# First attention by halves of its heads, block-diagonal keys in every score product, early weight rounding on ScalarE

## Chip, cores and metric

One core of a Trainium2 chip runs the kernel in one launch. The metric is the device time of an execution in microseconds (us).

## What is computed

A row of 256 positions and 1,024 features goes through two layers of a first block and two layers of a second, all in float32. The first block's layer 0 is an attention of 16 heads of 64 with a relative bias, its layer 1 a gated spatial mixing (gMLP); each is followed by a squared-ReLU feed-forward of 4,096. Shift, scale and gate of each come from a conditioning vector `c` through `ada_w` (6 × 1,024 columns per layer). The second block's layers hold, side by side, a differential attention (4 heads, two score maps of 64 each) and a grouped one (8 query heads, 2 key heads of 64).

```python
def first_block(...):
    for i in range(DEPTH):
        sh1, sc1, g1, sh2, sc2, g2 = split(silu(c) @ ada_w[i] + ada_b[i], 6)
        h = rms_norm(x, norm_mix[i]) * (1 + sc1) + sh1
        y = chunked_relpos_attention(h, ...) if i == 0 else chunked_spatial_gating(h, ...)
        x = x + g1 * y
        h = rms_norm(x, norm_ffn[i]) * (1 + sc2) + sh2
        x = x + g2 * (square(relu(h @ w1[i])) @ w2[i])

# attention: q, k, v = split(h @ w_in, 3); q, k normed per head of 64
#   s = q @ k.T + bias (chunks of 64, no later chunk); o = softmax(s) @ v; o @ w_out
# second block, per layer: proj = h @ w_in_2[l]
#   differential: a = softmax(q0 k0.T + bias) - lam * softmax(q1 k1.T + bias); a @ v
#   grouped: softmax(q k.T) @ v with 4 query heads to a key head; then @ w_out_2, norm, x + ...
```

## The kernel before, in words

**Products.** A float32 product is taken as three matmuls of rounded parts (`mm3`, L771 to L773): high by high, high by low, low by high. `mm` (L759) is a plain float32 matmul, which the chip runs as two records. `tr` (L799) is a transpose.

**Weights.** All weights lie in one stream, cut into items of 128 × 1,024 (0.5 MB), two items to a group; `stream_items` sets their order. `load_group` (L831) loads groups on the SP queue into four raw buffers. `item` then takes an item up: a weight for products is rounded to its high part (`hi`, L870 on ScalarE or L871 on VectorE) and VectorE subtracts for the low part (L873); the pair takes 2,048 columns of the rounded arena `R` (25,856 columns). `place` gives a pair out only while fewer than `NHL` = 9 live and `R` has 2,048 + `SPARE` columns free. Items `adc` and `adg` of `ada_w` go through VectorE alone (L737, L729).

**Order.** Each phase records operations with their dependencies; `Sched` then plays them on a model of the engines and writes one fixed order per engine, so a changed program moves instructions everywhere. An operation with two choices (`hi`, copies out of PSUM, scaled copies) goes to the engine that the planner picks. Four rounds are played and the best one is built.

**First stage** (`attention`). For each of eight k: two `adc` items give the scale and shift of 128 features, ScalarE forms h, `split` makes its high and low parts, and eight `mm3` of 512 columns add to eight PSUM banks (queries and keys of all 16 heads, two row tiles). Then v in two halves, the norms of all heads, and 16 heads one by one: a transposed query and key block per two heads, scores, softmax, transpose, times v. A head is 64 rows of a 128-row block, so its two score products (L759) use 64 rows. Last the output projection with the residual, then the transposes for the feed-forward layer (`norm_T`).

**Last two layers** (`block2`). Queries and keys of the differential heads come transposed out of `ws_block`; a head's two maps sit in rows 0 to 63 and 64 to 127 of one block, and each score product is an `mm3` over 64 rows and 256 columns. The grouped heads do the same with one key block for the two key heads. Projections of v and of the gates are meant to fill TensorE between the heads.

Of the kernel before, what the change touches and what calls it, by code (L numbers as in the profile page):

```python
# [13 lines left out]
ALU = mybir.AluOpType  # L14
# [44 lines left out]
def stream_items():  # L59
    s = []  # L60
    for k in range(KT):
        s += [("adc", 0, 1, k), ("adc", 0, 0, k), ("aqk", k, 0), ("aqk", k, 1)]
    s += [("av", h, q) for h in range(2) for q in range(4)]
    for x, y in ((ada_items(0, (2,)), ada_items(0, (4,))), (ada_items(0, (3,)), [("ao", k) for k in range(KT)])):
        for p in zip(x, y):
            s += p
# [28 lines left out]
def item_array(it, a):  # L95
# [7 lines left out]
    if n == "aqk":  # L103
        return a["a_w_in"][0][it[1] * P:(it[1] + 1) * P, it[2] * D:(it[2] + 1) * D]
    if n == "av":
        _, h, q = it
        w = a["a_w_in"][0][q * 256:(q + 1) * 256, 2 * D + h * 512:2 * D + (h + 1) * 512]
        return w.reshape(2, P, 512).transpose(1, 0, 2).reshape(P, D)
# [216 lines left out]
class Sched:  # L325
    AHEAD = 300
    NHL = 9
    SPARE = 2048
# [65 lines left out]
    def schedule(self, spaces, slots, rounds=4):  # L394
# [4 lines left out]
        for i in range(rounds):  # L399
            out = self.round(spaces, slots)  # L400
# [244 lines left out]
class Prog:  # L645
# [188 lines left out]
    def item(self):  # L834
# [30 lines left out]
        else:  # L865
# [4 lines left out]
            self.prev_split = S.op([("ACT", 0.093 + D / 1200.0, lambda: nc.scalar.copy(out=res(hi), in_=res(src))),  # L870
                                    ("DVE", 0.068 + D / 1920.0, lambda: nc.vector.tensor_copy(out=res(hi), in_=res(src)))],  # L871
                                   [src], [hi], after=after, pri=pri, kind=("hi", it))
# [100 lines left out]
    def split(self, hi, lo, src, n, psum=False, scale=1.0):  # L973
# [6 lines left out]
            [src, hi], [lo], kind="split_lo")  # L980

# [135 lines left out]
    def attention(self):  # L1117
# [3 lines left out]
        def load_bias(pri):  # L1121
            last = self.prev_dma
            for i in range(4):
# [5 lines left out]
        self.hooks[POS["adg", 0, 2, 0] // GRP] = [load_bias]  # L1129
# [21 lines left out]
        qk = [[self.F(D) for _ in range(2)] for _ in range(2)]  # L1151
        acc = {(t, n): self.bank((4 * t + n,)) for t in range(2) for n in range(4)}
        for k in range(KT):
            self.w("aqk", k, 0)
# [5 lines left out]
            for n, j in ([(n, j) for j in range(2) for n in range(2)] if k < KT - 1 else [(0, 0), (0, 1), (1, 0), (1, 1)]):  # L1160
                w = self.w("aqk", k, j)
                for t in range(2):
                    sl = slice(n * 512, (n + 1) * 512)
                    self.mm3(acc[t, 2 * j + n].v(), h0(k, t), (w[0][:, sl], w[1][:, sl]), 512, k == 0, k == KT - 1)
        for c in range(2):
            for t in range(2):
                for j in range(2):
                    self.copy(qk[t][j].v(c)[:, c * 512:(c + 1) * 512], acc[t, 2 * j + c].v(), 512, psum=True)
        v = [self.F(D) for _ in range(2)]

        def v_half(h):
            names = [("av", h, q) for q in range(4)]
            ps = [self.bank((0, 1, 2, 3)) for _ in range(2)]
            for k in range(KT):
                q, r = divmod(k, 2)
                w = self.w(*names[q])
                sl = slice(r * 512, (r + 1) * 512)
                for t in range(2):
                    self.mm3(ps[t].v(), h0(k, t), (w[0][:, sl], w[1][:, sl]), 512, k == 0, k == KT - 1)
            for t in range(2):  # L1180
                self.copy(v[t].v(h)[:, h * 512:(h + 1) * 512], ps[t].v(), 512, psum=True)

        v_half(0)
        S.bias += 400
        v_half(1)
        S.bias -= 400

        for n in range(2):
            hs = slice(n * 512, (n + 1) * 512)
            for t in range(2):  # L1190
                sq, ssq = self.F(D), self.F(16)
                for w in range(2):
                    self.act(sq.v(w)[:, w * 512:(w + 1) * 512], qk[t][w].v(n)[:, hs], 512, AF.Square)
                self.red(ssq.v(), sq.v().r("p (h d) -> p h d", h=16), D, ALU.add)
                r = self.rsqrt(ssq.v(), 16, 1.0 / 64, newton=True)
                for w in range(2):
                    v3 = qk[t][w].v(n)[:, hs].r("p (h d) -> p h d", h=8)
                    self.tt(v3, v3, r.v()[:, w * 8:(w + 1) * 8].u(2).bc(P, 8, 64), 512, ALU.mult)
        gqk = self.F(1)
        self.stt(gqk.v(), self.col("gq"), -0.125, self.col("gk"), 1, ALU.mult, ALU.mult)  # L1200
        self.load_group(POS["adg", 0, 2, 0] // GRP)
# [6 lines left out]
        qT, kT = {}, {}  # L1208
        osb = {}
        for h in range(16):  # L1210
            blk = h // 2
            if h % 2 == 0:
                ps = self.bank(TB)
                self.tr([ps.v()[:, (2 * w + t) * P:(2 * w + t + 1) * P] for w in range(2) for t in range(2)],
                        [qk[t][w].v(blk // 4)[:, blk * P:(blk + 1) * P] for w in range(2) for t in range(2)])
                qT[blk], kT[blk] = self.F(256), self.F(256)
                self.act(qT[blk].v(), ps.v()[:, 0:256], 256, scale=gqk.v(), psum=True, dve=True)
                self.copy(kT[blk].v(), ps.v()[:, 256:512], 256, psum=True)
            rr = slice((h % 2) * 64, (h % 2) * 64 + 64)
# [5 lines left out]
            for t, c, bc in ((1, slice(0, 256), slice(0, 256)), (0, slice(256, 384), slice(128, 256))):  # L1225
                n = c.stop - c.start
                self.ttr(p.v(t)[:, c], ps.v()[:, c], bias[:, bc], n, 3e38, ALU.add, ALU.min, m.v(t)[:, t:t + 1])
# [10 lines left out]
            vh = slice(h * 64, h * 64 + 64)  # L1238
            o = (h % 4) * 64
            key = h // 8  # L1240
            self.mm(ob.v()[:, 256 + o:320 + o], pT.v()[:, 0:P], v[0].v(key)[:, vh], 64, True, False)
            self.mm(ob.v()[:, 256 + o:320 + o], pT.v()[:, P:256], v[1].v(key)[:, vh], 64, False, True)
            self.mm(ob.v()[:, o:o + 64], pT.v()[:, 256:384], v[0].v(key)[:, vh], 64, True, True)
# [116 lines left out]
    def block2(self, l):  # L1360
# [3 lines left out]
        if l == 0:  # L1364
            self.nd = [self.F(2 * 384) for _ in range(2)]
# [72 lines left out]
        for c, sc in ((AQ, -0.125), (AK, 1.0)):  # L1438
            for i in range(4):
                ps = self.ws_block(hT, ("ws", l, c + 128 * i), (0, 1, 2, 3))  # L1440
                aT[c, i] = self.R(256), self.R(256)
# [10 lines left out]
        bkT = self.R(256), self.R(256)  # L1452
        self.split(bkT[0].v(), bkT[1].v(), ps.v()[:, 0:256], 256, psum=True)
# [22 lines left out]
        for t in range(2):  # L1476
            ob = self.bank(OB)
            for h in range(4):
                p, m, w = self.F(512), self.F(2), self.F(1)
                for c in range(2):  # L1480
                    ps = self.bank(SB)
# [5 lines left out]
                    self.ttr(pc, ps.v()[:, 0:256], self.nd[h // 2].v()[:, o:o + 256], 256, 3e38, ALU.add, ALU.min,  # L1487
# [27 lines left out]
        for t in range(2):  # L1515
            ob = self.bank(OB)
            for i in range(4):
                p, m = self.F(512), self.F(2)
                for g in range(2):
                    ps = self.bank(SB)  # L1520
                    rr = slice(g * 64, g * 64 + 64)
# [112 lines left out]
```

## Time and profile before

| what | value |
|---|---|
| median of 3 runs | 1012.61 us (1011.96 to 1013.88) |
| profiled execution, its own time | 1012.26 us |
| its span, first to last instruction | 1009.8 us |
| HBM read | 214.48 MB |
| DMA engines, mean busy share of q1 | 56.0% |
| chain that ended last | PE 82%, DVE 11%, ACT 3%, DMA 2% |

PE is TensorE's matmul, PEld its weight load, DVE VectorE, ACT ScalarE, POOL GpSimd, SP the queue that loads weights. Busy time is the time covered by instructions; a matmul's end is modelled and reaches beyond the start of the next, so the pace of TensorE is read from the starts. The profiled execution's own time is 2.5 us longer than its span, by what lies around it.

### The profile page before, as it was taken

What the parts mean: (1) busy time and instruction counts of PE and PEld (TensorE: products, weight loads), DVE (VectorE), ACT (ScalarE), POOL (GpSimd) and SP (SyncE); (2) the same over time, 40 slices, a digit from 0 to 9 for tenths busy, and PEclk for the clock granted to TensorE, in tenths of its full rate; (3) what the DMA queues carried; (4) which work ended last, traced back from release to release, by engine and by line L of the source; (5) the groups of instructions that cost most, each with busy time, mean ns of one, the idle gap of its engine ahead of it and who ended that gap; (6) DMA issues with size and microseconds to landing.
All of it is one profiled execution on the core that took longest, in us unless ns stands there. A gap on an engine that the chain in (4) does not pass through costs nothing.

```text
span 1009.8 us, 15115 instructions
## 1 busy us (share of the span) xinstructions
PE 984.2 (97%) x5844; PEld 856.1 (85%) x5844; DVE 767.9 (76%) x1319; ACT 576.7 (57%) x1045; POOL 18.5 (2%) x36
## 2 busy tenths in 40 slices
PE   6999988999999999999999999999999999999997
PEld 5887777899999888999998899999889788897786
DVE  6999999999778976876667855565696666985753
ACT  6376846545455656744445744455474576854873
POOL 0001000000000000000000000010000000000000
PEclk9999998999999999999999999999999999999999
DMA  9994595999776495776543545575455242453101
GB/s 351 368 369 168 209 374 191 359 377 342 276 289 222 159 370 202 299 253 247 195 181 134 200 167 188 187 271 176 164 188 187 87 154 84 167 208 126 43 1 42
DMA packets 32119, 216.50 MB, mean 214 GB/s; under 512 B 3824, under 2 KB 4080, under 8 KB 7216
## 3 DMA queue, kind: packets, MB, share of 16 engines
q1 hardware_dynamic: 30816, 211.98, 56.0%
q0 software_dynamic: 1232, 3.56, 1.4%
q8 instruction: 46, 0.75, 0.3%
q14 instruction: 25, 0.20, 0.1%
HBM read 214.48 MB, written 1.05 MB: 213 GB/s over the span
## 4 chain that ended last, share of the span: by engine, by line
PE 82%; DVE 11%; ACT 3%; DMA 2%; issue 2%; SPq 0%; DVEq 0%; ACTq 0%
PE banks L771 25%; PE banks L773 24%; PE banks L772 24%; PE banks L759 5%; DVE arena_r L873 4%; PE banks L799 3%; DVE arena L729 2%; DVE arena L737 2%; DMA raw<-in_wall 1%; ACT arena L684 1%; DVE arena L710 1%; DVE arena_r L978 1%; ACT arena_r L870 1%; DVE arena_r L871 1%; ACT arena L699 0%
## 5 line engine op out<-in xcount | busy, mean ns | idle before, releaser
L771 PE MATMUL banks<-arena_r 128*128 128x512 f32 (+2 forms) x1664 | 569.0, 345 | 3.3 <-ACT arena_r L976 3.0
L772 PE MATMUL banks<-arena_r 128*128 128x512 f32 (+2 forms) x1664 | 554.3, 336 | 0.0
L773 PE MATMUL banks<-arena_r 128*128 128x512 f32 (+2 forms) x1664 | 553.9, 335 | 0.4 <-DVE arena_r L978 0.4
L873 DVE TENSOR_TENSOR arena_r<-raw,arena_r 128x1024 fp32r<-128x1024 f32 x300 | 362.8, 1222 | 91.5 <-ACT arena_r L870 88.4
L870 ACT CAST arena_r<-raw 128x1024 fp32r<-128x1024 f32 x270 | 281.2, 1047 | 182.7 <-PE banks L773 77.8
L771 PEld LDWEIGHTS banks<-arena_r 128*128 128x128 f32 (+1 forms) x1664 | 313.8, 190 | 47.8 <-issue 7.9
L773 PEld LDWEIGHTS banks<-arena_r 128*128 128x128 f32 (+1 forms) x1664 | 313.6, 190 | 34.3 <-DVE arena_r L978 1.8
L772 PEld LDWEIGHTS banks<-arena_r 128*128 128x128 f32 (+1 forms) x1664 | 314.3, 190 | 28.8
L684 ACT ACTIVATE arena<-arena 128x256 f32<-128x256 f32 (+8 forms) x160 | 66.4, 422 | 47.5 <-DVE arena L737 17.4
L976 ACT ACTIVATE arena_r<-arena 128x256 fp32r<-128x256 f32 (+1 forms) x120 | 55.9, 475 | 51.6 <-DVE arena L729 35.2
L759 PE MATMUL banks<-arena 128*128 128x64 f32 (+4 forms) x480 | 72.3, 292 | 5.0 <-DMA arena<-in_ident 3.8
L737 DVE CUSTOM_DVE_ANT_0 arena<-raw,arena 128x1024 f32<-128x1024 f32 x56 | 71.8, 1281 | 6.6 <-DMA raw<-in_wall 3.8
L759 PEld LDWEIGHTS banks<-arena 128*128 128x128 f32 (+1 forms) x480 | 62.8, 195 | 14.7 <-ACT arena L699 4.2
L684 ACT ACTIVATE arena<-banks 128x256 f32<-128x256 f32 (+1 forms) x104 | 44.7, 431 | 51.7 <-PE banks L773 49.9
L799 PE MATMUL banks<-arena 128*128 128x128 f32 x356 | 57.0, 285 | 11.1 <-ACT arena L958 4.9
L978 DVE SCALAR_TENSOR_TENSOR arena_r<-arena,arena_r 128x256 fp32r<-128x256 f32 (+1 forms) x120 | 58.1, 492 | 9.7 <-ACT arena_r L976 9.1
L699 ACT COPY arena<-banks 128x512 f32<-128x512 f32 (+2 forms) x93 | 46.0, 502 | 32.4 <-PE banks L799 16.7
L799 PEld LDWEIGHTS banks<-arena 128*128 128x128 f32 x356 | 43.5, 148 | 21.3 <-ACT arena L958 6.3
L710 DVE TENSOR_TENSOR arena<-arena 128x512 f32<-128x512 f32 (+6 forms) x128 | 51.4, 434 | 7.2 <-ACT arena L684 5.8
L729 DVE SCALAR_TENSOR_TENSOR arena<-raw,arena 128x1024 f32<-128x1024 f32 x40 | 51.3, 1282 | 6.6 <-DMA raw<-in_wall 6.2
L729 DVE SCALAR_TENSOR_TENSOR arena<-banks,arena 128x256 f32<-128x256 f32 (+1 forms) x84 | 37.9, 451 | 21.9 <-PE banks L759 13.1
L710 DVE TENSOR_TENSOR arena<-banks,arena 128x512 f32<-128x512 f32 (+1 forms) x48 | 29.8, 642 | 16.4 <-PE banks L773 7.5
(44 smaller groups left out, 315.7 us busy)
## 6 DMA issues: line engine op xcount, KB each, us to landing
raw<-in_wall SPq DMA_DIRECT2D x194, 1024.0 KB, 4.9
raw<-in_wall SPq DMA_DIRECT2D x8, 512.0 KB, 9.1
arena<-in_nbias SPq DMA_DIRECT2D x4, 512.0 KB, 8.3
arena<-in_rows POOLq DMA_DIRECT2D x3, 512.0 KB, 6.8
arena<-in_xin SPq DMA_DIRECT2D x2, 512.0 KB, 5.7
out_dram<-arena SPq DMA_DIRECT2D x4, 256.0 KB, 2.5
arena<-in_dbias POOLq DMA_DIRECT2D x2, 384.0 KB, 6.4
arena<-in_wsT POOLq DMA_DIRECT2D x1, 512.0 KB, 3.8
```

Source lines behind the costliest of these rows:

```text
L684: nc.scalar.activation(out=res(out), in_=res(in_), func=func, scale=res(scale), **kw, **({"accum_out": res(accum)} if accum is not None el ...
L710: alt = ("DVE", 0.068 + n / 960.0, lambda: nc.vector.tensor_tensor(out=res(out), in0=res(a), in1=res(b), op=op))
L729: return self.S.op(("DVE", dur, lambda: nc.vector.scalar_tensor_tensor(out=res(out), in0=res(a), scalar=res(s), in1=res(b), op0=op0, op1=o ...
L737: return self.S.op(("DVE", dur, lambda: nc.vector.tensor_tensor_reduce(out=res(junk if out is None else out), in0=res(a), in1=res(b), scal ...
L759: o = self.S.op(("PE", max(n, 96) * 0.00167, lambda: nc.tensor.matmul(res(out), lhsT=res(l), rhs=res(r), start=start, stop=stop)), rd, [ou ...
L771: nc.tensor.matmul(o, lhsT=lh, rhs=rh, start=start, stop=False)
L772: nc.tensor.matmul(o, lhsT=lh, rhs=rl, start=False, stop=False)
L773: nc.tensor.matmul(o, lhsT=ll, rhs=rh, start=False, stop=stop)
L799: nc.tensor.transpose(res(o), res(i), res(ident))
L870: self.prev_split = S.op([("ACT", 0.093 + D / 1200.0, lambda: nc.scalar.copy(out=res(hi), in_=res(src))), ("DVE", 0.068 + D / 1920.0, lamb ...
L873: dve = ("DVE", 0.068 + D / 960.0, lambda: nc.vector.tensor_tensor(out=res(lo), in0=res(src), in1=res(hi.f32()), op=ALU.subtract))
L978: self.S.op(("DVE", 0.068 + n / 960.0, lambda: nc.vector.scalar_tensor_tensor(out=res(lo), in0=res(src), scalar=scale, in1=res(hi.f32()), ...
```

## The change

1. *First attention by halves of heads.* In the k loop only the first eight heads' queries, keys and values are projected (six `mm3` per k and three banks per row tile). Items `aqk` hold both halves' 512 columns, `a2` the values and the second half. The second half's three projections are recorded between the first half's norms and its heads, with a priority that lets them fill in (`S.bias`). The bias tables load two and two.
2. *Block-diagonal keys.* Two 64-row key blocks are written into the two diagonal blocks of a 128 × 512 buffer whose other blocks are zeroed once. One product over 128 rows gives the scores of two heads (or of two maps). In `block2` the ten buffers of 512 columns are fixed in `R`; maxima of the grouped heads are taken for two heads at once.
3. *Early roundings.* Items ahead of the first feed-forward weight are rounded on ScalarE alone.
4. *Planner.* `SPARE` 2,048 to 5,120; a round that finds no operation to start ends the search.

```diff
-        s += [("adc", 0, 1, k), ("adc", 0, 0, k), ("aqk", k, 0), ("aqk", k, 1)]
-    s += [("av", h, q) for h in range(2) for q in range(4)]
+        s += [("adc", 0, 1, k), ("adc", 0, 0, k), ("aqk", k)]
+        if k % 2 == 0:
+            s.append(("a2", 2, 0, k // 2))
+    for x, y in ((ada_items(0, (2, 4)), [("a2", j, 1, q) for j in range(3) for q in range(4)]),
+                 (ada_items(0, (3,)), [("ao", k) for k in range(KT)])):
...
-    SPARE = 2048
+    SPARE = 5120
...
+            self.prev_split = S.op(alts[:1] if i < POS["w1", 0, 0] else alts, [src], [hi], after=after, pri=pri,
+                                   kind=("hi", it))
...
+    def split_diag(self, kd, ps):
+        for c in range(2):
+            rr, cc = slice(c * 64, c * 64 + 64), slice(c * 256, (c + 1) * 256)
+            self.split(kd[0].v(c)[rr, cc], kd[1].v(c)[rr, cc], ps.v()[rr, 0:256], 256, psum=True)
...
+        norms(0)
+        S.bias += 300
+        for j in range(3):
+            second(j)
+        S.bias -= 300
...
-            self.mm(ps.v()[:, 0:256], qT[blk].v()[rr, P:256], kT[blk].v()[rr, :], 256, True, True, 0.5)
-            self.mm(ps.v()[:, 256:384], qT[blk].v()[rr, 0:P], kT[blk].v()[rr, 0:P], P, True, True, 0.5)
+                self.mm(s1.v(), qT.v()[:, P:256], kk.v(), 512, True, True)
+                self.mm(s0.v()[:, 0:256], qT.v()[:, 0:P], kk.v().r("p (g k) -> p g k", g=2)[:, :, 0:P], 256, True, True)
...
+            self.kd = [(self.R(512), self.R(512)) for _ in range(5)]
...
-                    ps = self.bank(SB)
-                    rr = slice(c * 64, c * 64 + 64)
-                    self.mm3(ps.v()[:, 0:256], tuple(b.v()[rr, t * P:(t + 1) * P] for b in aT[AQ, h]),
-                             tuple(b.v()[rr, :] for b in aT[AK, h]), 256, True, True, 0.5)
+                ps = self.bank(SB)
+                self.mm3(ps.v(), tuple(b.v()[:, t * P:(t + 1) * P] for b in aT[AQ, h]), tuple(b.v() for b in self.kd[h]),
+                         512, True, True)
...
+                self.red(m.v(), ps.v().r("p (g k) -> p g k", g=2), 512, ALU.max)
```

What the planner makes of it, engine by engine. Lines of the changed kernel stand 10 or 11 lower: L739 is the old L729, L747 the old L737, L769 the old L759, L781 to L783 the old L771 to L773, L809 the old L799, L884 the old L873, L989 the old L978.

VectorE in the middle of the k loop, before (L737 takes an `adc` item, L729 of one column its gain, L871 rounds, L873 subtracts, L978 is the low part of h):

```order
L729 SCALAR_TENSOR_TENSOR arena<-arena 128x1
L871 CAST arena_r<-raw 128x1024
L873 TENSOR_TENSOR arena_r<-raw,arena_r 128x1024 x2
L978 SCALAR_TENSOR_TENSOR arena_r<-arena,arena_r 128x256
L737 ISA arena<-raw,arena 128x1024
L737 ISA arena 128x1
L737 ISA arena<-raw,arena 128x1024
```

The same place in the changed kernel:

```order
L739 SCALAR_TENSOR_TENSOR arena<-arena 128x1
L884 TENSOR_TENSOR arena_r<-raw,arena_r 128x1024
L989 SCALAR_TENSOR_TENSOR arena_r<-arena,arena_r 128x256
L747 ISA arena<-raw,arena 128x1024
L747 ISA arena 128x1
L747 ISA arena<-raw,arena 128x1024
L747 ISA arena 128x1
L884 TENSOR_TENSOR arena_r<-raw,arena_r 128x1024
```

The rounding is gone from VectorE, and a step holds one or two subtractions in place of two.

TensorE where the scores of the first `block2` layer begin, before (the products of 256 columns are scores over 64 rows, those of 512 columns projections):

```order
L799 MATMUL banks<-arena 128x128 x2
L771 MATMUL banks<-arena_r 128x256
L772 MATMUL banks<-arena_r 128x256
L773 MATMUL banks<-arena_r 128x256
L771 MATMUL banks<-arena_r 128x512
L772 MATMUL banks<-arena_r 128x512
L773 MATMUL banks<-arena_r 128x512
```

The same place in the changed kernel:

```order
L809 MATMUL banks<-arena 128x128 x2
L781 MATMUL banks<-arena_r 128x512
L782 MATMUL banks<-arena_r 128x512
L783 MATMUL banks<-arena_r 128x512
L781 MATMUL banks<-arena_r 128x512
L782 MATMUL banks<-arena_r 128x512
L783 MATMUL banks<-arena_r 128x512
```

No product of 256 columns is left among the heads: scores are as wide as the projections between them.

TensorE at the end of the first stage, before (L759 of one column sums the shift of the feed-forward layer, the products are the output projection's):

```order
L771 MATMUL banks<-arena_r 128x512
L772 MATMUL banks<-arena_r 128x512
L773 MATMUL banks<-arena_r 128x512
L759 MATMUL banks<-arena 128x1 x8
L771 MATMUL banks<-arena_r 128x512
L772 MATMUL banks<-arena_r 128x512
L773 MATMUL banks<-arena_r 128x512
```

In the changed kernel (L809 are the transposes for the feed-forward layer, of the first row tile and of the second):

```order
L783 MATMUL banks<-arena_r 128x512
L809 MATMUL banks<-arena 128x128 x8
L769 MATMUL banks<-arena 128x1 x8
L809 MATMUL banks<-arena 128x128 x8
L781 MATMUL banks<-arena_r 128x512
```

The column sums moved from the middle of the output projection to between the two sets of transposes.

## Rows read from the trace of the kernel before

**Rows 1.** The page: busy us, share of the span, instructions of each engine.

```profile
PE 984.2 (97%) x5844; PEld 856.1 (85%) x5844; DVE 767.9 (76%) x1319; ACT 576.7 (57%) x1045; POOL 18.5 (2%) x36
```

**Rows 2.** Windows: stretch, length, busy time per engine (instructions), granted clock, DMA share, GB/s.

```profile
20.00:40.00 20.00, 20.00 (x85) 16.40 (x85) 19.26 (x30) 8.26 (x12) 0.00 (x0) 1.00 0.99 389
...
800.00:820.00 20.00, 19.72 (x114) 15.52 (x113) 17.77 (x49) 14.16 (x37) 1.06 (x2) 1.00 0.33 96
...
880.00:900.00 20.00, 20.00 (x148) 19.04 (x147) 19.93 (x42) 13.65 (x24) 0.00 (x0) 1.00 0.57 214
```

**Rows 3.** Chain of waits, one step of the k loop: start us, us, what.

```profile
28.46 1.22 DVE arena L737 x2
...
31.07 0.61 DVE arena_r L871
31.70 2.36 DVE arena_r L873 x2
...
34.40 1.21 DVE arena L737 x2
```

**Rows 4.** Groups by shape, first 157 us: count, busy us, mean ns, idle before.

```profile
L873 DVE TENSOR_TENSOR arena_r<-raw,arena_r 128x1024 fp32r<-128x1024 f32 x34 | 40.7, 1221 | 1.3 <-ACT arena_r L870 0.9
...
L871 DVE CAST arena_r<-raw 128x1024 fp32r<-128x1024 f32 x14 | 9.5, 688 | 0.0
...
L978 DVE SCALAR_TENSOR_TENSOR arena_r<-arena,arena_r 128x256 fp32r<-128x256 f32 x8 | 3.4, 420 | 0.0
...
L702 DVE COPY arena<-banks 128x512 f32<-128x512 f32 x1 | 0.7, 685 | 0.0
...
L870 ACT CAST arena_r<-raw 128x1024 fp32r<-128x1024 f32 x25 | 26.2, 1050 | 17.5 <-DMA raw<-in_wall 17.5
```

**Rows 5.** Timeline of TensorE, first `block2` layer: start us, us, engine, line, rows*columns, shape.

```profile
783.55 0.40 PE L773 MATMUL banks<-arena_r 128*128 128x512 f32 x1
783.88 0.38 PE L771 MATMUL banks<-arena_r 64*128 64x256 f32 x1
784.10 0.28 PE L772 MATMUL banks<-arena_r 64*128 64x256 f32 x1
784.22 0.27 PE L773 MATMUL banks<-arena_r 64*128 64x256 f32 x1
784.42 0.50 PE L771 MATMUL banks<-arena_r 128*128 128x512 f32 x1
784.76 0.39 PE L772 MATMUL banks<-arena_r 128*128 128x512 f32 x1
784.99 0.39 PE L773 MATMUL banks<-arena_r 128*128 128x512 f32 x1
```

**Rows 6.** The same view, a stretch of three products, the first two side by side.

```profile
817.40 0.39 PE L771 MATMUL banks<-arena_r 64*128 64x256 f32 x2
817.62 0.29 PE L772 MATMUL banks<-arena_r 64*128 64x256 f32 x2
817.74 0.29 PE L773 MATMUL banks<-arena_r 64*128 64x256 f32 x2
817.86 0.28 PE L771 MATMUL banks<-arena_r 64*128 64x256 f32 x1
```

**Rows 7.** Groups by shape, 760 to 1010 us: the 64-row products.

```profile
L771 PE MATMUL banks<-arena_r 64*128 64x256 f32 x64 | 18.3, 378 | 0.2 <-DVE arena L737 0.2
```

**Rows 8.** Timeline of TensorE: the first and the last of the stretches of 64-row work.

```profile
781.74 0.38 PE L771 MATMUL banks<-arena_r 64*128 64x256 f32 x1
...
979.34 0.38 PE L771 MATMUL banks<-arena_r 64*128 64x256 f32 x1
```

**Rows 9.** Timeline of TensorE, first stage: scores of two heads, and of one.

```profile
80.84 0.93 PE L759 MATMUL banks<-arena 64*128 64x256 f32 x8
...
108.99 0.92 PE L759 MATMUL banks<-arena 64*128 64x256 f32 x4
```

**Rows 10.** Timeline of TensorE after the output projection: transposes for the feed-forward layer.

```profile
150.90 1.21 PE L799 MATMUL banks<-arena 128*128 128x128 f32 x8 [2.79 <-DVE arena L956]
```

More of the change, by code (lines that the diff above doesn't have):

```diff
@@ L103, in item_array @@
     if n == "aqk":
[L104 to L107, printed above, removed]
+        w = a["a_w_in"][0][it[1] * P:(it[1] + 1) * P]
+        return np.concatenate([w[:, 0:512], w[:, D:D + 512]], axis=1)
+    if n == "a2":
+        _, j, h, q = it
+        w = a["a_w_in"][0][q * 256:(q + 1) * 256, j * D + h * 512:j * D + (h + 1) * 512]
         return w.reshape(2, P, 512).transpose(1, 0, 2).reshape(P, D)
@@ L399, in schedule @@
         for i in range(rounds):
-            out = self.round(spaces, slots)
+            try:
+                out = self.round(spaces, slots)
+            except RuntimeError:
+                if best is None:
+                    raise
+                break
             if best is None or self.clock < best[0]:
@@ L1119, in attention, with load_bias @@
         nb = [self.F(4 * 256) for _ in range(4)]
-        def load_bias(pri):
+        def load_bias(pri, which):
             last = self.prev_dma
-            for i in range(4):
+            for i in which:
                 last = S.op(("SP", 1.46, lambda i=i: nc.sync.dma_start(
@@ L1127, in load_bias @@
             return last
-        self.hooks[POS["adg", 0, 2, 0] // GRP] = [load_bias]
+        for it, which in ((("a2", 0, 1, 0), (0, 1)), (("a2", 2, 1, 0), (2, 3))):
+            self.hooks[POS[it] // GRP] = [lambda pri, which=which: load_bias(pri, which)]
+        kd = [self.F(512) for _ in range(2)]
+        for b in kd:
+            for c in range(2):
+                self.memset(b.v(2 + c)[(1 - c) * 64:(2 - c) * 64, c * 256:(c + 1) * 256], 0.0, 256)
         for g in range(2):
@@ L1159, in attention, with second @@
             self.split(hT[0][k].v(), hT[1][k].v(), f.v(), 256)
-            for n, j in ([(n, j) for j in range(2) for n in range(2)] if k < KT - 1 else [(0, 0), (0, 1), (1, 0), (1, 1)]):
-                w = self.w("aqk", k, j)
+            for j in range(3):
                 for t in range(2):
-                    sl = slice(n * 512, (n + 1) * 512)
-                    self.mm3(acc[t, 2 * j + n].v(), h0(k, t), (w[0][:, sl], w[1][:, sl]), 512, k == 0, k == KT - 1)
-        for c in range(2):
+                    sl = slice(j * 512, (j + 1) * 512) if j < 2 else slice((k % 2) * 512, (k % 2 + 1) * 512)
+                    w = wqk if j < 2 else wv
+                    self.mm3(acc[t, j].v(), h0(k, t), (w[0][:, sl], w[1][:, sl]), 512, k == 0, k == KT - 1)
+        for j in range(3):
             for t in range(2):
[L1167 to L1173, printed above, removed]
+                self.copy(qkv[j][0][t].v(), acc[t, j].v(), 512, psum=True)
+        def second(j):
+            ps = [self.bank((0, 1, 2)) for _ in range(2)]
             for k in range(KT):
-                q, r = divmod(k, 2)
-                w = self.w(*names[q])
-                sl = slice(r * 512, (r + 1) * 512)
+                w = self.w("a2", j, 1, k // 2)
+                sl = slice((k % 2) * 512, (k % 2 + 1) * 512)
                 for t in range(2):
@@ L1180, in v_half, with norms @@
             for t in range(2):
[L1181 to L1189, printed above, removed]
+                self.copy(qkv[j][1][t].v(), ps[t].v(), 512, psum=True)
+        def norms(n):
             for t in range(2):
@@ L1237, in attention @@
                 ob = self.bank(OB)
-            vh = slice(h * 64, h * 64 + 64)
+            v = [qkv[2][h // 8][t].v()[:, (h % 8) * 64:(h % 8 + 1) * 64] for t in range(2)]
             o = (h % 4) * 64
[L1240 to L1243, printed above, removed]
+            self.mm(ob.v()[:, 256 + o:320 + o], pT.v()[:, 0:P], v[0], 64, True, False)
+            self.mm(ob.v()[:, 256 + o:320 + o], pT.v()[:, P:256], v[1], 64, False, True)
+            self.mm(ob.v()[:, o:o + 64], pT.v()[:, 256:384], v[0], 64, True, True)
             if h % 4 == 3:
@@ L1364, in block2 @@
         if l == 0:
+            self.kd = [(self.R(512), self.R(512)) for _ in range(5)]
+            for kd in self.kd:
+                for b in kd:
+                    for c in range(2):
+                        self.memset(b.v(2 + c)[(1 - c) * 64:(2 - c) * 64, c * 256:(c + 1) * 256].f32(), 0.0, 256)
             self.nd = [self.F(2 * 384) for _ in range(2)]
@@ L1451, in block2 @@
         self.tr([ps.v()[:, t * P:(t + 1) * P] for t in range(2)], [kr[t].v() for t in range(2)])
[L1452 to L1453 removed]
+        self.split_diag(self.kd[4], ps)
         av, sg, sb = {}, {}, {}
```

71 lines of the change are left out of this document (39 added, 32 removed).

## The prediction

> **What bounds the kernel now.** I read the page first: TensorE is busy 97% of the span, VectorE 76%, ScalarE 57% [rows 1]. A busy TensorE need not be a TensorE at its best, so the windows come next: from 20 us on it is busy in practically every microsecond at a granted clock of 1.00 (2.4 GHz), in the first stage as in the last two layers, and VectorE stands beside it at 19.26 of 20 us in the first stage, 17.77 and 19.93 in two windows of the last layers [rows 2]. So time goes only where TensorE's own work shrinks, or, in the first 150 us, where both get shorter. The chain of waits over the first projections runs on VectorE: one step of the k loop starts at 28.46 and the next at 34.40, 5.94 us [rows 3]. The timeline of TensorE in the last two layers shows where it works badly: every score product with a 64-row stationary costs far more than its columns [rows 5, 6].
>
> **The change, part by part.**
>
> *Score products of the two last layers (block2).* Before, 64 products of three matmuls, 64 rows by 256 columns [rows 7]. The plain pace is 0.23 us for a 128-row matmul of 512 columns and 0.12 for one of 256. Around a 64-row product the starts are 0.33, 0.22, 0.12, 0.20 and 0.34 us apart, 1.21 us from the product ahead to the second matmul of the one behind, where 0.23 + 3 × 0.12 + 0.23 = 0.82 would do [rows 5]. Each stretch of 64-row work thus pays 0.39 us for going in and out, and takes 0.36 + 0.39 = 0.75 us. I counted the stretches in the timeline from the first to the last: 42 [rows 8]. 37 hold one product, or two that run at once (below); the other five hold more and take about 0.46 us longer each (a further product is 0.36, a second pair 0.46). Sum before: 42 × 0.75 + 5 × 0.46 = 33.8 us. After, 32 products of three 128-row matmuls of 512 columns, 3 × 0.23 = 0.69 us each: 22.1 us. TensorE saves **11.7 us**. All of it lies on the path as long as TensorE is the bound there.
>
> Some 64-row products come in neighbouring pairs, one in each half of the rows, and then run at once: the first two products start together at 817.40 and are through at 817.86, 0.46 us for two, while the third takes 0.36 by itself [rows 6]. The Trainium skill ("TensorEngine Tiling (Array Packing)", Overview, Theoretical Speedup) says that a contraction of at most 64 rows can win up to 2x by row tiling. By that rule alone 64 products are 32 pairs of 0.36 us, 11.5 us in all, and the block-diagonal form would lose 10.6 us instead of winning 11.7. The trace bears the overlap out, yet the 42 stretches as they stand cost 33.8 us, because 0.39 us is paid each time. I take the measured sum.
>
> *What else moves there.* The split of the keys doubles its instructions: five more on ScalarE and five on VectorE per layer, of 0.42 us [rows 4]. Eight pairs of maxima per layer become one each. Both nearly cancel on VectorE and lie beside TensorE; if that cover were gone they would cost 2 us per layer. The fixed key buffers take 10 × 512 = 5,120 columns of the rounded arena, and the spare went from 2,048 to 5,120. In block2 hT 4,096, queries 2,048 and 2,048 and the ones 128 are live besides; a weight pair of 2,048 is given out while 2,048 plus the spare is free. Before (keys 2,048 + 512): 14,976 free, six pairs. After: 12,416 free, three pairs. Three is enough on the average: a pair costs 1.05 us on ScalarE and 1.22 on VectorE [rows 4], and feeds four products, 2.8 us. But TensorE reaches a layer's start and its output projection with less in hand. Bounds: 0, and 2.3 us for each of eight pairs. I take **+1.5 us**, near the low end, since even two pairs in turn keep up.
>
> *First stage, the k loop.* ScalarE alone now rounds the early weights. A step loses one rounding on VectorE (31.07 to 31.70, 0.63 us) and half a subtraction (two take 2.36 with the rest, so 0.59) [rows 3]: 5.94 − 0.63 − 0.59 = 4.7 us. TensorE's part of a step falls from 24 matmuls to 18, 4.1 us. So eight steps take 38 us instead of 47.5, but TensorE idles 0.6 us in each, up to 4.8 us in all; the products displaced (48 matmuls) return behind. DMA carries 3.5 items of 0.52 MB per step, 390 GB/s, against 389 reached in the window [rows 2]: just enough, and a reason why the step may be 4.8.
>
> *First stage, the rest.* Up to the gating of the residual VectorE does 11 roundings fewer (11 × 0.61 = 6.7 us; 0.69 us by the group, 0.61 back to back [rows 4]), but the planner gives it more copies out of PSUM: six more of 512 columns at 0.685, two of 384, two more scaled and one half copy of 256, less two of 256, which by columns is 5.5 us, and one more sum of squares of 512, 0.7. Net −0.5 us. ScalarE gains what VectorE lost; it is busy 57% and has room, though an exponential can stand behind a 1.05 us rounding that waits for its weights. The 16 heads' scores: 13 stretches of 64-row work before, 0.93 us each whether one head or two (a pair 0.93, one head 0.92 [rows 9]): 12.1 us. A head's columns without the switch are about 0.6 us, and full-row products of 16 heads have as many: 16 × 0.62 = 9.9. TensorE −2.2. So TensorE's sum is −2.2 + 4.8 = +2.6 at worst, VectorE's −0.5. The stage ended on VectorE (TensorE waited 2.79 us for it at 150.90 [rows 10]), so I take a value nearer to it, **+0.6 us**, with bounds −3 (both gains, none of the idle time) and +4 (the idle time and the next sentence). In the handover to the feed-forward layer the shift's column sums now stand between the two transposes; they delay the first tile by about 1 us but no longer split the second from its products: 0.
>
> The bias loads are two groups of two on the SP queue instead of four together; the weights behind them wait for 1 MB twice instead of 2 MB once, with up to eight raw items landed ahead. The zeroing of the key buffers sits on POOL, 2% busy. Both nothing. The layers between (feed-forward, gMLP) keep their TensorE work.
>
> Sum, against the profiled execution (1012.26 us, span 1009.8, 0.35 below the median): 1012.3 − 11.7 + 1.5 + 0.6 = **1002.7 us**.
>
> **The rivals.**
> - *The first stage wins too.* Shorter steps and no 64-row switches, and the second half's projections fill what the heads leave: −3 there, and the waits of block2 go as well (−1.5): 998 us. For it: the chain lies on VectorE [rows 3]. Against: VectorE's sum hardly moves. Chance 0.14.
> - *The first stage loses.* TensorE's idle 4.8 us is not made good, and ScalarE's roundings delay exponentials: +4, 1006 us. For it: TensorE was full in 20 to 40 us [rows 2]. Chance 0.13.
> - *VectorE and ScalarE set the pace in block2.* With 11.7 us less on TensorE the windows of 17.77 and 19.93 [rows 2] become the bound and most of the gain turns into waits: 1010 us. Chance 0.10.
> - *Slower: starved of weights.* If in block2 fewer than two pairs fit at a time, each pair of an output projection is rounded only after the one before is used up: 1.05 + 1.22 = 2.27 us of idle TensorE, 8 × 2.27 = 18 in one layer: 1021 us. It decides from four such waits on (9 us). Against: three pairs by the sum above. Chance 0.10.
> - *Slower: row halves were worth more than the switches.* The mechanism of neighbouring pairs: if the 42 stretches hid their switches under other work, 32 × 0.69 replaces 11.5 us: about 1025 us. Against: the starts show the switches [rows 5]. This is the rule named above; it gets 0.03.
> - *The change isn't in the program*: excluded, the order shows it.
>
> **How the numbers follow.** The forecast, 1002.7, has 0.50. The range takes in the first-stage rivals and most of the third, and the starvation up to about five waits: 995 to 1013, about 8 in 10. About 0.2%, 2 us, is what a measurement of this kernel can tell from no change. Faster: 0.50 + 0.14 + 0.13 and a bit of the third, 0.78. Same: 0.08. Slower: 0.14.
>
> **What would show it.** Right: no 64-row matmul is left; between a score product and its neighbours the starts are 0.23 us; the first layer of block2 to the end takes about 10 us less from its first norm on, and the transposes ahead of the feed-forward layer start within 4 us of 150.90. Wrong: TensorE idle on a subtraction or rounding of weights in block2 for more than 6 us, or a granted clock below 1.00 in the k loop, or those transposes later than 156.

## The result, and the profile after

| | before | after |
|---|---|---|
| median | 1013.23 us (4 runs, 1011.96 to 1013.88) | 1004.79 us (4 runs, from 1002.91) |
| profiled execution, own time | 1012.26 us | 1004.64 us |
| its span | 1009.8 us | 1002.8 us |

The ratio is 0.9913, 95% interval 0.9896 to 0.9929: 8.4 us faster, where 9.9 below the earlier median was forecast (1002.7, range 995 to 1013). One of the four runs after, at 1072.55 us, was disturbed: it counts in that median, which is 1004.64 without it, and in no ratio. Of the gain, 7.0 us lie inside the span; the time around the span fell from 2.5 to 1.8 us, which no run explains. In the changed kernel the roundings on ScalarE stand at L880.

The page of the changed kernel, busy us by engine, answers to [rows 1]:

```profile
PE 974.5 (97%) x5716; PEld 853.4 (85%) x5716; DVE 775.9 (77%) x1306; ACT 568.1 (57%) x1052; POOL 24.8 (2%) x60
```

TensorE's share is as before, and 9.7 us of its busy time are gone. The groups by shape from 776 us to the end (count, busy us, mean ns, idle before) answer to [rows 7]:

```profile
L781 PE MATMUL banks<-arena_r 128*128 128x512 f32 x208 | 87.7, 422 | 2.6 <-ACT arena_r L987 2.6
...
L809 PE MATMUL banks<-arena 128*128 128x128 f32 x164 | 25.4, 273 | 0.4 <-DVE arena_r L989 0.4
L783 PE MATMUL banks<-arena_r 128*128 128x256 f32 x88 | 24.9, 283 | 0.0
```

No 64-row group is left; products of 512 columns went from 176 to 208, the 32 that were forecast. TensorE waits for no weights here: 2.6 and 0.4 us are all its waits, and both are for parts of h (L987 and L989). Scores are now as wide as the projections, and matmuls of 512 columns start 0.23 us apart among themselves, 0.32 right behind the transposes:

```profile
785.69 0.38 PE L809 MATMUL banks<-arena 128*128 128x128 f32 x2
785.82 0.48 PE L781 MATMUL banks<-arena_r 128*128 128x512 f32 x1
786.14 0.40 PE L782 MATMUL banks<-arena_r 128*128 128x512 f32 x1
786.37 0.40 PE L783 MATMUL banks<-arena_r 128*128 128x512 f32 x1
786.61 0.40 PE L781 MATMUL banks<-arena_r 128*128 128x512 f32 x1
```

The windows (as [rows 2], and two more) show where it is not full:

```profile
20.00:40.00 20.00, 18.10 (x79) 14.58 (x77) 18.40 (x29) 9.97 (x14) 0.00 (x0) 0.99 0.90 363
40.00:60.00 20.00, 18.68 (x72) 14.23 (x72) 16.73 (x25) 15.10 (x26) 0.62 (x2) 0.91 0.94 368
800.00:820.00 20.00, 20.00 (x110) 16.59 (x109) 17.38 (x43) 15.58 (x37) 0.00 (x0) 1.00 0.30 106
860.00:880.00 20.00, 17.41 (x76) 14.09 (x75) 18.90 (x30) 12.80 (x29) 0.00 (x0) 0.83 0.38 135
880.00:900.00 20.00, 20.00 (x155) 19.39 (x154) 17.18 (x40) 11.12 (x21) 0.00 (x0) 1.00 0.57 194
```

The stretch from 20 to 60 us, the k loop and what follows it, now has holes. In 860 to 880, where the first of the last two layers hands over to the second, TensorE loses 2.6 us and the granted clock is 0.83. TensorE's timeline there:

```profile
863.78 0.39 PE L783 MATMUL banks<-arena_r 128*128 128x512 f32 x1
864.01 1.04 PE L809 MATMUL banks<-arena 128*128 128x128 f32 x8
867.64 0.79 PE L781 MATMUL banks<-arena_r 128*128 128x512 f32 x1 [2.59 <-ACT arena_r L987]
868.23 0.63 PE L782 MATMUL banks<-arena_r 128*128 128x512 f32 x1
868.66 0.63 PE L783 MATMUL banks<-arena_r 128*128 128x512 f32 x1
...
873.78 0.44 PE L783 MATMUL banks<-arena_r 128*128 128x512 f32 x1
874.06 1.04 PE L809 MATMUL banks<-arena 128*128 128x128 f32 x8
```

At 864.01 stand the transposes of the first row tile for the next layer, at 874.06 those of the second. Between them lie 10.05 us with only five products (15 matmuls, 3.4 us at the plain pace): the second tile is being normalized, and the order holds nothing else there. In the kernel before 16 products of 512 columns stand between these transposes, and TensorE waits nowhere:

```profile
865.49 1.07 PE L799 MATMUL banks<-arena 128*128 128x128 f32 x8
...
877.73 1.10 PE L799 MATMUL banks<-arena 128*128 128x128 f32 x8
```

The first stage hardly moved. The chain of waits from 26 us on, and the transposes and first product of the feed-forward layer, which answer to [rows 3, 10]:

```profile
25.60 1.29 DVE arena L747 x2
28.05 8.32 DMA raw<-in_wall
36.50 1.31 DVE arena L747 x2
```

```profile
149.43 1.09 PE L809 MATMUL banks<-arena 128*128 128x128 f32 x8 [0.52 <-DVE arena L967]
...
154.35 1.97 PE L809 MATMUL banks<-arena 128*128 128x128 f32 x8 [2.15 <-DVE arena L967]
155.97 0.78 PE L781 MATMUL banks<-arena_r 128*128 128x512 f32 x1
```

The longest piece of the whole chain is now 8.32 us of weights arriving. The transposes start 1.5 us earlier than in [rows 10]; the first feed-forward layer ends at 335.90 instead of 336.59, and the last two layers start at 778.64 instead of 779.17. So 0.5 of the 7.0 us of span come from everything up to there, 6.5 from the last two layers.

### The profile page after: what moved, and what is told of

It reads as the page before. It is cut to its first block, busy times and chain, and to the rows that moved or that the text cites. A ratio compares the mean times of both kernels' runs of the same rounds, so it can differ in the third digit from the quotient of the medians.

```text
span 1002.8 us, 14856 instructions
## 1 busy us (share of the span) xinstructions
PE 974.5 (97%) x5716; PEld 853.4 (85%) x5716; DVE 775.9 (77%) x1306; ACT 568.1 (57%) x1052; POOL 24.8 (2%) x60
## 4 chain that ended last, share of the span: by engine, by line
PE 83%; DVE 9%; DMA 3%; ACT 3%; issue 2%; SPq 0%; DVEq 0%; ACTq 0%
PE banks L781 26%; PE banks L782 26%; PE banks L783 25%; PE banks L769 4%; DVE arena_r L884 3%; PE banks L809 3%; DMA raw<-in_wall 2%; DVE arena L747 2%; DVE arena L720 1%; DVE arena L739 1%; DVE arena_r L989 1%; DMA arena<-in_xin 1%; ACT arena L694 1%; ACT arena_r L880 1%; ACT arena L709 0%
## 5 line engine op out<-in xcount | busy, mean ns | idle before, releaser
L781 PE MATMUL banks<-arena_r 128*128 128x512 f32 (+1 forms) x1632 | 564.8, 346 | 3.5 <-ACT arena_r L987 3.5
L782 PE MATMUL banks<-arena_r 128*128 128x512 f32 (+1 forms) x1632 | 554.7, 340 | 3.8 <-DVE arena_r L884 3.5
L783 PE MATMUL banks<-arena_r 128*128 128x512 f32 (+1 forms) x1632 | 553.6, 339 | 0.0
L884 DVE TENSOR_TENSOR arena_r<-raw,arena_r 128x1024 fp32r<-128x1024 f32 x300 | 360.1, 1221 | 43.8 <-ACT arena_r L880 42.5
L782 PEld LDWEIGHTS banks<-arena_r 128*128 128x128 f32 x1632 | 311.6, 191 | 36.7 <-DVE arena_r L884 6.3
L781 PEld LDWEIGHTS banks<-arena_r 128*128 128x128 f32 x1632 | 311.5, 191 | 35.1 <-ACT arena_r L987 4.1
L783 PEld LDWEIGHTS banks<-arena_r 128*128 128x128 f32 x1632 | 310.9, 191 | 35.7 <-DVE arena_r L989 1.3
L880 ACT CAST arena_r<-raw 128x1024 fp32r<-128x1024 f32 x268 | 274.4, 1044 | 81.7 <-DMA raw<-in_wall 42.4
L987 ACT ACTIVATE arena_r<-arena 128x256 fp32r<-128x256 f32 (+1 forms) x120 | 55.9, 475 | 87.5 <-DVE arena L739 55.9
L747 DVE CUSTOM_DVE_ANT_0 arena<-raw,arena 128x1024 f32<-128x1024 f32 x56 | 71.7, 1281 | 13.6 <-DMA raw<-in_wall 12.0
L739 DVE SCALAR_TENSOR_TENSOR arena<-banks,arena 128x256 f32<-128x256 f32 (+1 forms) x84 | 37.8, 452 | 52.1 <-ACT arena L694 37.3
L989 DVE SCALAR_TENSOR_TENSOR arena_r<-arena,arena_r 128x256 fp32r<-128x256 f32 (+1 forms) x120 | 58.3, 494 | 25.5 <-ACT arena_r L987 24.3
L769 PE MATMUL banks<-arena 128*128 128x64 f32 (+4 forms) x448 | 70.0, 291 | 4.2 <-DMA arena<-in_ident 3.8
L769 PEld LDWEIGHTS banks<-arena 128*128 128x128 f32 x448 | 60.3, 195 | 11.1 <-ACT arena L694 3.8
L809 PE MATMUL banks<-arena 128*128 128x128 f32 x356 | 56.5, 285 | 10.8 <-DVE arena L730 4.6
L809 PEld LDWEIGHTS banks<-arena 128*128 128x128 f32 x356 | 44.6, 148 | 23.9 <-DVE arena L730 4.8
L709 ACT COPY arena<-banks 128x512 f32<-128x512 f32 (+4 forms) x95 | 45.4, 484 | 29.5 <-PE banks L809 17.1
L739 DVE SCALAR_TENSOR_TENSOR arena<-raw,arena 128x1024 f32<-128x1024 f32 x40 | 51.2, 1280 | 3.9 <-DMA raw<-in_wall 3.6
```

The lines of the kernel that those rows point to most:

```text
L739: return self.S.op(("DVE", dur, lambda: nc.vector.scalar_tensor_tensor(out=res(out), in0=res(a), scalar=res(s), in1=res(b), op0=op0, op1=o ...
L747: return self.S.op(("DVE", dur, lambda: nc.vector.tensor_tensor_reduce(out=res(junk if out is None else out), in0=res(a), in1=res(b), scal ...
L769: o = self.S.op(("PE", max(n, 96) * 0.00167, lambda: nc.tensor.matmul(res(out), lhsT=res(l), rhs=res(r), start=start, stop=stop)), rd, [ou ...
L781: nc.tensor.matmul(o, lhsT=lh, rhs=rh, start=start, stop=False)
L782: nc.tensor.matmul(o, lhsT=lh, rhs=rl, start=False, stop=False)
L783: nc.tensor.matmul(o, lhsT=ll, rhs=rh, start=False, stop=stop)
```

## The experiments

**Each part alone.** `b2_only` is the kernel before with `split_diag`, the full-row products of `block2` and the larger reserve; `att_only` has the rest: the first attention and the early roundings.

```diff
 b2_only
-    SPARE = 2048
+    SPARE = 5120
...
+                if c == AK:
+                    self.split_diag(self.kd[i], ps)
+                    continue
...
```

> The kernel before with only the block-diagonal keys of the last two layers (and the larger reserve they need). Theory 1 (the gain comes from the last two layers, less what the layer boundary gives back): 1006 to 1008 us, that is 5.5 to 7.5 below the kernel before, with the last two layers at 223 to 226 us instead of 230.6, and the same hole at the boundary between them (TensorE idle about 2.5 us, then some 13 products at the 1.2 GHz level). Theory 2 (half or more of the gain comes from the first attention): 1010 us or more.

Measured: 1006.8 us, ratio 0.9939 (0.9926 to 0.9951). The last two layers take 225.2 us. There is a hole at the boundary, but not quite the same one: most of it stands ahead of the first tile's transposes, and most matmuls of the five products behind them start 0.43 us apart.

```profile
868.39 1.39 PE L804 MATMUL banks<-arena 128*128 128x128 f32 x8 [3.29 <-DVE arena L961]
```

> The kernel before with only the change of the first attention (halves of heads, block-diagonal first keys, early roundings on ScalarE); the last two layers and the reserve as before. Theory 1: 1012 to 1013.5 us, within 1 us of the kernel before, since the first attention and the stage ahead of it end only 0.5 to 1.5 us earlier. Theory 2: 1009 us or less.

Measured: 1013.21 us, ratio 0.9998 (0.9990 to 1.0007). Theory 1 holds: most of the gain is the last two layers', and the first attention with the early roundings brings nothing alone. Its transposes do start sooner, 148.60 against 150.90, but the 2.3 us are lost 20 us later. TensorE and then ScalarE in that kernel:

```profile
171.50 0.66 PE L809 MATMUL banks<-arena 128*128 128x128 f32 x4 [2.84 <-ACT arena L709]
```

```profile
169.91 1.04 ACT L880 CAST arena_r<-raw 128x1024 fp32r<-128x1024 f32 x1 [3.25 <-DMA raw<-in_wall]
170.86 0.58 ACT L709 COPY arena<-banks 128x512 f32<-128x512 f32 x1
```

A copy that TensorE waits for stands on ScalarE behind a rounding whose weights have not landed.

**Switch or count?** `full_rows_256` keeps 64 products of 256 columns, but over all 128 rows.

```diff
 full_rows_256
-                ps = self.bank(SB)
-                self.mm3(ps.v(), tuple(b.v()[:, t * P:(t + 1) * P] for b in aT[AQ, h]), tuple(b.v() for b in self.kd[h]),
-                         512, True, True)
                 for c in range(2):
+                    ps = self.bank(SB)
+                    self.mm3(ps.v()[:, 0:256], tuple(b.v()[:, t * P:(t + 1) * P] for b in aT[AQ, h]),
+                             tuple(b.v()[:, c * 256:(c + 1) * 256] for b in self.kd[h]), 256, True, True)
...
```

> The changed kernel with every block-diagonal score product of the last two layers cut into two of 256 columns, in banks of their own as before: all 128 rows, as many matmuls of as many columns as the kernel before has in 64 rows. Theory 1 (the cost of before is the change of the row count at each stretch's ends): the last two layers take 223 to 227 us and the whole 1004 to 1007 us, as the changed kernel. Theory 3 (the saving comes from half as many matmuls, or from one reduction and one bank in place of two): most of the gain goes, 1009 us or more, the last two layers 228 us or more.

Measured: 1005.45 us, ratio 0.9922 (0.9910 to 0.9933); the last two layers take 224.7 us, the changed kernel's 224.2. The number of matmuls, banks and reductions is worth at most 0.5 us here. What went is the change of the row count.

**The hole at the layer boundary.** In `fresh_keys` the key buffers are taken and zeroed in each layer, so their 5,120 columns are free for weight pairs in between.

```diff
 fresh_keys
+        self.kd = [(self.R(512), self.R(512)) for _ in range(5)]
...
         if l == 0:
...
-            self.kd = [(self.R(512), self.R(512)) for _ in range(5)]
...
```

> The changed kernel with the key buffers of the last two layers taken anew in each layer instead of kept over both, so that their 5120 columns are free for weight pairs while one layer hands over to the next. Theory A (the hole at the layer boundary comes from the scarcity of weight pairs, which forces the second row tile's output products ahead of the first tile's transposes): the wait of 2.59 us at 867.64 and the products at the 1.2 GHz level go, 999.5 to 1002 us, 3 to 5.5 below the changed kernel's 1004.8. Theory B (the hole comes from the shorter attention itself, whatever the memory): 1004 to 1005.5 us with the hole in its place.

Measured: 1000.25 us, ratio 0.9877 (0.9860 to 0.9893). TensorE's timeline and the window there:

```profile
860.94 0.60 PE L809 MATMUL banks<-arena 128*128 128x128 f32 x4
861.30 0.48 PE L781 MATMUL banks<-arena_r 128*128 128x512 f32 x1
...
862.08 0.60 PE L809 MATMUL banks<-arena 128*128 128x128 f32 x4
862.44 0.48 PE L781 MATMUL banks<-arena_r 128*128 128x512 f32 x1
...
869.96 0.66 PE L809 MATMUL banks<-arena 128*128 128x128 f32 x4
```

```profile
860.00:880.00 20.00, 19.85 (x107) 16.18 (x106) 18.31 (x28) 14.21 (x30) 0.00 (x0) 1.00 0.46 158
```

The second tile's transposes come 9.02 us after the first's, not far from the changed kernel's 10.05, but eleven products instead of five fill the time. The last two layers take 219.1 us. Most of that gain is at the boundary: counted from the starts, in the stretch 75 to 105 us into these layers TensorE loses 5.9 us against its usual gaps in the changed kernel, 1.3 here and 0.5 in the kernel before.

`tail_4` reaches the same place without more memory: only the last four weight pairs are used tile by tile, and eight products are left between the two tiles' transposes.

```diff
 tail_4
-TAIL_ATT, TAIL_B2 = 6, (8, 6)
+TAIL_ATT, TAIL_B2 = 6, (4, 6)
```

> The changed kernel with the output projection of the last but one layer written so that 4 instead of 8 of its products per half come tile by tile (the last 4 weight pairs, not all 8, must be held until the first tile is done). The order then has 8 instead of 5 products between the two tiles' transposes. Theory A (missing filler makes the hole): the hole of 2.59 us of idle and 13 products at the 1.2 GHz level shrinks, 1001.5 to 1004 us. Theory B: 1004 to 1005.5 us.

Measured: 1001.71 us, ratio 0.9892 (0.9877 to 0.9906), the wait 1.54 us, the last two layers 220.9.

`b2_fresh` is `b2_only` with `fresh_keys`' edit; here the planned order keeps its few fillers, six, in spite of the free columns.

> The kernel before with the block-diagonal keys of the last two layers alone, in buffers taken anew in each layer. Here the planner still puts 27 products ahead of the first tile's transposes at the layer boundary and 6 between the two tiles' (19 + 1 ahead and 10 after both in the fresh_keys kernel). If the hole follows the order (no filler beside the second tile's normalization): it stays, 1004 to 1008 us. If it follows the columns that are free: it goes, 1001 to 1003 us.

Measured: 1006.85 us, ratio 0.9947 (0.9926 to 0.9967), with a wait of 1.92 us at 873.25. With the columns free and only six fillers a hole stays, so free columns alone do not fill it. It is smaller, though: the last two layers take 221.9 us, 3.3 less than in `b2_only`. The time that was forecast came by another way, since these layers start only at 785.51: the new order starts the first feed-forward layer's transposes at 156.57. So this run separates order and memory in part only.

`reserve_alone` is the kernel before with one number changed (and the planner ending its search where a round does not fit).

```diff
 reserve_alone
-    SPARE = 2048
+    SPARE = 5120
...
```

> The kernel before with only the reserve raised from 2048 to 5120 columns (and the planner's guard for a round that does not fit), which leaves fewer places for weight pairs. If thin weights cost by themselves: 1014 to 1018 us, with the loss at the boundary between the last two layers, where 8 products instead of 16 are left between the two row tiles' transposes. If only the keys' own buffers make the pairs too few: within 1.5 us of the kernel before.

Measured: 1013.79 us, ratio 1.0010 (1.0001 to 1.0019): within the bound of 1.5 us, so a thin reserve without the keys costs little. Its last two layers take 232.0 us, 1.4 more than before, with nine products between the two tiles' transposes and a wait of 1.02 us ahead of them. Whether the fixed keys with the old reserve do better was not run.

**Once more side by side.** No edit; the changed kernel and `fresh_keys` again.

> The changed kernel itself, timed once more beside fresh_again on one chip: 1003.5 to 1005.5 us.

Measured: 1005.6 us, ratio 0.9926 (0.9911 to 0.9940), 0.1 above what was expected.

> The fresh_keys kernel once more, beside the changed kernel on one chip. Theory A: 3 to 5.5 us below after_again. If the first comparison was chance: within 1.5 us of it.

Measured: 1001.45 us, ratio 0.9877 (0.9859 to 0.9896), 4.2 us less. `fresh_keys` is the fastest version found. TensorE at the boundary in this second execution of the changed kernel:

```profile
866.55 0.71 PE L809 MATMUL banks<-arena 128*128 128x128 f32 x5
...
870.18 0.50 PE L781 MATMUL banks<-arena_r 128*128 128x512 f32 x1 [2.59 <-ACT arena_r L987]
870.52 0.39 PE L782 MATMUL banks<-arena_r 128*128 128x512 f32 x1
...
876.02 1.10 PE L809 MATMUL banks<-arena 128*128 128x128 f32 x8 [1.84 <-DVE arena L967]
```

The wait of 2.59 us is the same, but the five products now run at the plain pace, and the second tile is waited for instead: 9.47 us from tile to tile, against 10.05. The low clock of the first execution cost little by itself. Here TensorE waits for the second tile's normalization, there it is held by its own slower matmuls, to nearly the same length; only filler can use the time.

**The first stage.** `both_engines_cast` takes the third part of the change back; `casts_alone` is that part alone on the kernel before.

```diff
 both_engines_cast
...
-            self.prev_split = S.op(alts[:1] if i < POS["w1", 0, 0] else alts, [src], [hi], after=after, pri=pri,
-                                   kind=("hi", it))
+            self.prev_split = S.op([("ACT", 0.093 + D / 1200.0, lambda: nc.scalar.copy(out=res(hi), in_=res(src))),
+                                    ("DVE", 0.068 + D / 1920.0, lambda: nc.vector.tensor_copy(out=res(hi), in_=res(src)))],
+                                   [src], [hi], after=after, pri=pri, kind=("hi", it))
```

> The changed kernel without its third part: the early roundings may go to ScalarE or VectorE, as before. Theory V: up to 14 roundings of 0.69 us go back to VectorE in the first 157 us, the first FFN's transposes start 2 to 9 us later than 149.43 and the whole takes 1007 to 1014 us. Theory D (what VectorE saves there is lost in waits for weights anyway): 1004 to 1006 us.

Measured: 1012.14 us, ratio 0.9989 (0.9980 to 0.9998), seven of the eight us. In the profiled execution (1010.04, the fastest of its runs) the feed-forward transposes start at 153.28 and the last two layers, 224.3 us long as after, at 783.96. Little of this can be VectorE's roundings: the planner put 5 on VectorE in the first 157 us, where the changed kernel has 1 and the kernel before 14. Of the 5.5 us of span over the changed kernel 3.5 are there when the first feed-forward layer ends, and 1.8 come in the layers between, whose weights the edit leaves alone.

> The kernel before with only the third part of the change: the early weights' roundings on ScalarE alone. Theory P (VectorE's relief pays only where the rest of the first stage is ordered around it): 1011 to 1014 us, no gain. Theory Q (the roundings are what the first stage gains by, since putting them back cost 7.3 us in the changed kernel): 1005 to 1009 us.

Measured: 1016.39 us, ratio 1.0067 (1.0036 to 1.0098): slower, which neither theory had. Its ten runs spread from 1014.23 to 1028.63, so the size of the loss is uncertain. The profiled execution, the fastest, took 1014.23 us with the first stage as before (150.62) and the last two layers at 232.5, 1.9 more than before, far from the roundings.

`thin_ada` leaves VectorE's products of the first gates and scales out but for 64 columns:

```diff
 thin_ada
-            self.stt(acc, src, c, acc, D, ALU.mult, ALU.add)
+            n = 64 if i < POS["w1", 0, 0] else D
+            self.stt(acc[:, 0:n], src[:, 0:n], c, acc[:, 0:n], n, ALU.mult, ALU.add)
```

> The changed kernel with the 16 VectorE products of 1024 columns that build the first layer's gates and scales by rows ahead of the first FFN cut to 64 columns (so those gates and scales are left out but for 64 columns; every transfer and every rounding stays): some 16 x (1.28 - 0.14) = 18 us of VectorE go from the first 157 us. Theory V (VectorE, 94 to 97% busy, paces the first stage, so TensorE time saved there shows nowhere): the transposes ahead of the first FFN, 149.43 now, start at 146 or sooner and the first FFN ends at 332 or sooner (335.90 now). Theory D (the arrival of the weights paces it): both within 2 us of where they are.

Measured: 1003.35 us, ratio 0.9904 (0.9891 to 0.9917). The first transposes do start at 145.40, as theory V had it, but the first product of the layer and the second tile's transposes do not follow:

```profile
153.83 0.80 PE L781 MATMUL banks<-arena_r 128*128 128x512 f32 x1 [2.97 <-ACT arena_r L988]
...
156.77 1.91 PE L809 MATMUL banks<-arena 128*128 128x128 f32 x8
```

The first feed-forward layer ends at 335.81, against 335.90. 18 us less on VectorE are worth some 2 us: theory V's second sign fails. Theory D is not shown by that either, since `both_engines_cast` misses what it expected and meets what V expected.

## Why the prediction was right, and where not

**The score products of the last two layers: −11.7, right in mechanism and size.** The time from the transposes ahead of these layers to the end, by kernel:

| score products | kernels | us |
|---|---|---|
| 64 rows | before, `att_only`, `reserve_alone`, `casts_alone` | 230.6, 230.8, 232.0, 232.5 |
| 128 rows, boundary with a hole | after, `after_again`, `full_rows_256`, `both_engines_cast`, `thin_ada`, `b2_only` | 224.2, 223.7, 224.7, 224.3, 223.5, 225.2 |
| 128 rows, hole partly or wholly filled | `b2_fresh`, `tail_4`, `fresh_keys`, `fresh_again` | 221.9, 220.9, 219.1, 219.1 |

With the hole filled, 230.6 − 219.1 = 11.5 us. Taken one by one from the starts in the trace, the 42 stretches take 34.7 us, against 33.8 by the sum, and `full_rows_256` shows that the row count was the cause. The Trainium skill ("TensorEngine Tiling (Array Packing)", Tiling Modes, Key Properties) says that a change of tiling mode drains TensorE; these runs agree in that a change of the row count costs 0.39 us a stretch by [rows 5]. The rival by the rule on row tiling, at 1025 us, did not come: the halves can overlap [rows 6], which saves 0.26 us for a pair, less than the 0.39 us at a stretch's ends. One sign of being right was set too high by the forecast's own sum: these layers took 6.5 us less, where about 10 were named.

**The thin weight pairs: +1.5, mis-sized and elsewhere.** The fixed key buffers measured 224.2 − 219.1 = 5.1 us, and this is the step that failed. It was looked for as TensorE waiting for roundings; no such wait came, so the rival of four starved waits and its sign were both wrong about the form. "Three is enough on the average" holds on the average. But the output projection wants all eight of its pairs held until the first row tile is done, and with fewer places the *order* changes (argued from the code): 28 products stand ahead of the first tile's transposes, and the second tile's normalization then stands bare. `fresh_keys` and `tail_4` show that filler brings the time back, with memory and without; `b2_fresh` shows that free columns alone do not bring all of it.

**The first stage: +0.6, within what can be told, the parts not.** `att_only` is at 0.9998. The transposes started at 149.43 in one execution of the changed kernel and at 151.71 in the other, so its 1.5 us of gain are no finding. The parts of the term were less good. The last row-wise product of the k loop starts at 48.09 us instead of 53.46, 5.4 us sooner and not 9.5. The weights came at 363 and 368 GB/s in the two windows and not at 390, and 8.32 us of the chain are a wait for them; whether DMA was at its limit or loads started late, behind buffers that VectorE frees, is not shown. And a sign named as wrong did appear, a granted clock of 0.91 in 40 to 60 us; in the other execution it was 1.00, and the layer ended no sooner for it. That VectorE ends this stage is not borne out: `thin_ada` takes 18 us from it, the first transposes start 4.0 us sooner, and the layer's end moves by 0.1.

**The early roundings: counted inside that term, and open.** Taken back they cost 7 us, though only four roundings moved; alone they cost 3.7 by the median and 1.8 by the span of the profiled execution, instead of winning. Single parts do not add: −6.3 for `b2_only` and 0 for `att_only`, −8.4 for the whole. Every kernel gets a new order everywhere: the first stages of `b2_only` and `b2_fresh` are the same code, and their feed-forward transposes start at 150.84 and 156.57. Which share of the 7 us is ScalarE's rounding and which the order's luck stays open.

**The handover and the queues: 0, borne out within a microsecond.** The second tile's transposes come 3.2 us sooner and the first product 1.75 later; the layer's end moves by 0.7. No run looks at the queues alone. One reading was too smooth: TensorE of the kernel before was not busy all through, but idle 2.79, 2.11 and 0.44 us at this handover.

**The sum, with some luck.** By the profiled executions the last two layers gave 6.5 us where 11.7 − 1.5 = 10.2 were forecast, a miss of 3.7. Everything ahead of them gave 0.5 where a loss of 0.6 was forecast, and 0.6 came from outside the span, where nothing was forecast. So the total missed by only 1.9 us (1004.64 against 1002.7).

## What to carry to other kernels

Where a short product uses half the rows between full-row work, count the stretches and the pace lost at their ends, not the columns; zero-padded full rows can win. A buffer held over stages that don't need it costs even if nobody waits for memory, because it can take the filler work away from a layer boundary. When one planner orders everything, trust a part's price only if a row shows it: the total of a kernel with one part undone also holds a new order.

## What was not expected of the hardware

After the same idle time of 2.59 us at the boundary, TensorE came back with matmuls 0.43 us apart (512 columns, the 1.2 GHz level, granted clock 0.83 in the window) in one execution and 0.23 to 0.24 us apart after the first few (1.00) in the other. The low level cost only 0.6 us from tile to tile (10.05 against 9.47), since in the other execution TensorE waited 1.84 us for VectorE at the end.
